# Hybrid diffusion backbone on one core: conditioning dots moved from the attention to the merge, and norms in two VectorE operations per block

## Chip, cores, metric

The kernel runs on one core of one Trainium2 chip. The metric is the device time of one execution in microseconds (us); three runs of the kernel before gave a median of 2265.24 us (2264.16 to 2270.03).

## What is computed

Two layers of a token mixer and an MLP on 512 latent tokens of width 1024, with 256 context tokens as a prefix that goes through the same weights. All is fp32. Cut to what matters here:

```python
for l in range(2):
    mod = silu(c) @ w_ada[l] + b_ada[l]          # 6 x 1024 columns; the same with c_ctx for the context
    sh1, sc1, g1, sh2, sc2, g2 = split(mod, 6)
    h = rms_norm(x, norm1[l]) * (1 + sc1) + sh1
    u, q, k, v, ..., gates = project(h @ w_in[l])
    y_pool, y_swa, y_diff = pool_mixer(u), windowed_gqa(...), diff_attention(...)
    merged = sum(sigmoid(gate_b) * (y_b @ w_b) for b in (pool, swa, diff))
    x = x + g1 * (merged @ w_out[l])
    h2 = rms_norm(x, norm2[l]) * (1 + sc2) + sh2
    x = x + g2 * (relu(h2 @ w_ff1[l])**2 @ w_ff2[l])
    # the context does the same in layer 0
```

The 6144 values of `mod` are 48 columns of 128: 0 to 7 are sh1, 8 to 15 sc1, 16 to 23 g1, 24 to 31 sh2, 32 to 39 sc2, 40 to 47 g2.

## The kernel before

**Layout and precision.** Activations lie transposed: eight blocks of 128 rows of the width, with 768 token columns (512 latent, 256 context). A matmul keeps fp32 precision by three passes: every operand is a pair of tiles, the value rounded to the matmul's format (the high half, written by ScalarE) and the remainder (the low half, a subtraction). The products high x high, low x high and high x low go into one PSUM tile (lines 231 to 233, 1014 to 1016, 396). Weights stream through SyncE's queue as tiles of 768 columns (`raw`, 384 KB, line 190) and are split into `W` on the way: high half on ScalarE (line 172), low half (line 173) on VectorE, or on GpSimd where the caller passes an engine. Three raw and six split tiles are in flight. A tile holds six weight blocks of 128 x 128.

**Order of the work.** Per layer: first norm, attention (projections, windowed and differential attention, with gate units as filler), pooling branch, merge, output projection with the second norm, MLP. The order in the program is written out by hand (`ORDER`, `unit_plan`, `merge_plan`, `mlp_plan`); the order on each engine is planned from it at build time, with priorities (`PRI`, `HIGH`). Every engine and SyncE's queue then work in their order.

**Conditioning dots.** A column of `mod` is the dot of 128 rows of `w_ada` (a load of 512 KB, tile `wada`) with the activated conditioning vector, one for the latents and, in layer 0, one for the context: `tensor_tensor_reduce` over 1024 columns on VectorE. Columns 0 to 15 of layer 0 are made with matmuls in the prologue. Columns 16 to 39 of layer 0 run beside the attention of layer 0: `ada_attn` (lines 250 to 266, dot at line 264, load at line 262), a generator that `pump()` advances by one column, 24 columns over the first 30 of the attention's steps (line 910). The rest, columns 40 to 47 of layer 0 and all 48 of layer 1, runs in the MLP of layer 0: `ada` (lines 283 to 288, dot at line 279, load at line 270 and kept in program order), pumped by the feed-forward units (lines 1387 and 1395). `ada` first loads both conditioning vectors (`cvec`, line 244) and activates them (lines 238 and 239). Its weights have two buffers, those of `ada_attn` one.

**Merge** (lines 1279 to 1332). Five gate units (eight blocks each, 768 token columns in two groups, 48 matmuls by three passes) and 24 branch units (four blocks, 24 matmuls); each of them already calls `pump()`, which finds nothing to do there today. A branch unit's result is multiplied by its gate and added up on VectorE (lines 1317, 1321, 1324).

**Norms.** `norm_stats` gives the reciprocal root mean square, broadcast over the partitions in a PSUM tile `bc`: squares on ScalarE (line 310), their sum on VectorE (line 311), a sum over partitions by matmul (line 315), the power on GpSimd (line 180), a broadcast by transposes (line 321). `norm` (second norm, to tile `xn`) and `norm_apply` (first norm of layer 1, in place) multiply the eight blocks by `bc` (lines 354, 348). `modulate` then writes the high half of `h` on ScalarE with scale and bias (line 339), applies scale and shift on VectorE (line 340) and makes the low half (line 341) on VectorE for even blocks and on GpSimd for odd ones (`MODP`). The second norm runs in two halves, each behind its half of the output projection, whose results are added to x at line 1354. In layer 1's first norm the latents are normed while the context's last feed-forward units run in layer 0 (`next(mods)`, line 1403); the context's follow behind those. Of these last feed-forward units the weights' low halves, from line 1392, are made on GpSimd (`FE`).

Of the kernel before, what the change touches and what calls it, by code (L numbers as in the profile page):

```python
# [7 lines left out]
F32 = mybir.dt.float32  # L8
F32R = mybir.dt.float32r
BF16 = mybir.dt.bfloat16  # L10
AF = mybir.ActivationFunctionType
ALU = mybir.AluOpType
# [40 lines left out]
def merge_plan(l):  # L53

    g = (START[l] + sum(GATES_AT[l]))
    first = min(24, max(g, 16) + AHEAD)
    seq = [("gate", i) for i in range(g, first)]
    for i in range(24):
        if i >= 16 and first < 24:
            seq.append(("gate", first))  # L60
            first += 1
        seq.append(("br", i))
    return seq
# [45 lines left out]
HIGH = 100  # L109
OUTA = 1  # L110
OUTE = (None, None)
MODP = 2
PRE = ((0, 0), (0, 4))
YP = ()
MGP = ()
WG = (None, None)
WB = ((None, None), (None, None))
ATT = {"Q": 5, "E": 4, "PT": 3, "y": 2, "ph": 2, "zs": 3, "st": 6, "wada": 1}
ADA_ATTN = range(16, 40)
ADA_STEPS = 30  # L120
KVB = 6
MT = 4
ZC = True
FE = "pool"
LAG = 1
PW = "pool"
RAW = 3
# [8 lines left out]
class Kern:  # L136
# [196 lines left out]
            gs[:, k:k + 2], self.mod[l][:, v, j0 + k:j0 + k + 2], 1.0, self.col(l, norm0 + k, 2),  # L333
            ALU.add, ALU.mult)

    def modulate(self, t, h, k, a, b, gs, sh):

        nc = self.nc
        nc.scalar.activation(h[k][:, 0, a:b], t, AF.Identity, bias=sh[:, k:k + 1], scale=gs[:, k:k + 1])
        nc.vector.tensor_scalar(t, t, gs[:, k:k + 1], sh[:, k:k + 1], ALU.mult, ALU.add)  # L340
        (nc.gpsimd if k % MODP == 1 else nc.vector).tensor_tensor(
            h[k][:, 1, a:b], t, h[k][:, 0, a:b].bitcast(F32), op=ALU.subtract)

    def norm_apply(self, x, a, b):

        bc = self.norm_stats(x, a, b)
        for k in range(8):
            self.nc.vector.tensor_tensor(x[k][:, a:b], x[k][:, a:b], bc[:, 0:b - a], op=ALU.mult)

    def norm(self, x, h, a, b, gs, sh):  # L350
        bc = self.norm_stats(x, a, b)
        for k in range(8):
            t = self.T("xn")[:, 0:b - a]
            self.nc.vector.tensor_tensor(t, x[k][:, a:b], bc[:, 0:b - a], op=ALU.mult)
            self.modulate(t, h, k, a, b, gs, sh)

    def new_h(self, name, pool=None):
        return [(pool or self.hp).tile([128, 2, NT], F32R, tag="h", name=f"{name}{k}") for k in range(8)]
# [472 lines left out]
    def attention(self, l, h, tail):  # L831
# [53 lines left out]

        self.side = self.ada_attn(ADA_ATTN) if l == 0 else None
        for ti in range(6):
# [4 lines left out]
        for gi, (kind, i) in enumerate(items):  # L892
# [13 lines left out]
            for j, (a, subs) in enumerate(us):  # L906
                step(b, a, dd, subs, total * (j + 1) // len(us) - total * j // len(us))
                dd, b = b, a
                done += 1
                self.pump(done * len(ADA_ATTN) // ADA_STEPS - (done - 1) * len(ADA_ATTN) // ADA_STEPS)  # L910
            if gi == len(items) - 2:
# [287 lines left out]
    def run(self):  # L1199
        nc, tc, a, ctx = self.nc, self.tc, self.a, self.ctx  # L1200
        pool = lambda name, bufs=1, **kw: ctx.enter_context(tc.tile_pool(name=name, bufs=bufs, **kw))
# [31 lines left out]
        with tc.manual_schedule():  # L1233
            h = self.prologue(p0.__enter__())
        self.side = None
        prev_pool = p0
        x = None

        def first_norm(l, x, h, v):
            ga, gb = (lat, cx)[v]  # L1240
            gs = self.gains(l, v, 8, 0)
            self.norm_apply(x, ga, gb)
            yield
            for k in range(8):
                self.modulate(x[k][:, ga:gb], h, k, ga, gb, gs, self.mod[l][:, v, 0:8])
                yield

        for l in range(DEPTH):
# [3 lines left out]
            if l > 0:  # L1252
                d = self.first = self.group_w(l, "swa", 0, None)
                if PRE:
                    with tc.issue_after(self.last_mm.ins):
                        for t, k in PRE:
                            self.proj_mm(l, h, d, t, k, k + 4)
                for _ in first_norm(l, x, h, 1):
                    pass
# [21 lines left out]
            B = _Tagged(raw, {"tg": 8, "mg": 8})  # L1281
            self.tp = _Tagged(raw, {"T": 2})
            mg = [None] * 8
            mh = None
            tg = {}

            def gate(i):
                ps = self.s("gate")
                self.unit(ps, self.blocks(l, "gate", i, eng=WG[l]), h, groups)
                t = tg[i] = B.tile([128, NT], F32, tag="tg", name="tg")  # L1290
                nc.scalar.activation(t[:, 0:n], ps[:, 0:n], AF.Tanh, scale=0.5)
                self.pump()

            def tg_load(i):
                t = tg[i] = B.tile([128, NT], F32, tag="tg", name="tgl")
                nc.sync.dma_start(t[:, 0:n], self.tgd[i][:, 0:n])

            for name, i in merge_plan(l):
                if name == "gate":
                    gate(i)  # L1300
                    continue
                b, m = divmod(i, 8)
                if m == 0:
                    y = self.load_y((0, 2, 1)[b], n)
                    if b == 2:
                        mh = self.new_h("mh")
                if i < (START[l] + sum(GATES_AT[l])):
                    tg_load(i)
                if True:
                    ps = self.s("br")  # L1310
                    self.unit(ps, self.blocks(l, "br", i, eng=WB[l][i % 2]), y, groups)
                    t = tg.pop(i)
                    hi = tc.high_priority(offset=HIGH)
                    hi.__enter__()
                    if b == 0:
                        mg[m] = B.tile([128, NT], F32, tag="mg", name="mg")
                        nc.vector.scalar_tensor_tensor(mg[m][:, 0:n], t[:, 0:n], 1.0, ps[:, 0:n],
                                                       ALU.add, ALU.mult)
                        hi.__exit__(None, None, None)
                    else:  # L1320
                        nc.vector.scalar_tensor_tensor(t[:, 0:n], t[:, 0:n], 1.0, ps[:, 0:n],
                                                       ALU.add, ALU.mult)
                        hi.__exit__(None, None, None)
                        (nc.gpsimd if b in MGP else nc.vector).tensor_tensor(mg[m][:, 0:n], mg[m][:, 0:n], t[:, 0:n],
                                                                             op=ALU.add)
                    self.pump()
                    if b == 2:
                        nc.scalar.activation(mh[m][:, 0, 0:n], mg[m][:, 0:n], AF.Copy, scale=0.5)
                        nc.vector.scalar_tensor_tensor(mh[m][:, 1, 0:n], mg[m][:, 0:n], 0.5,
                                                       mh[m][:, 0, 0:n].bitcast(F32), ALU.mult, ALU.subtract)  # L1330
            pb.__exit__(None, None, None)
            pk.__exit__(None, None, None)

# [5 lines left out]
            x = []  # L1339
            for k in range(8):  # L1340
                t = M.tile([128, NT], F32, tag="x", name="x")
# [6 lines left out]
            for turn, (ga, gb) in enumerate(halves):  # L1348
                v = turn if l == 0 else 0
# [7 lines left out]
                if l == 0 or turn == 0:  # L1357
                    gs = self.gains(l, v, 32, 8)
                self.norm(x, h2, ga, gb, gs, self.mod[l][:, v, 24:32])
            if l == 0:  # L1360
                pc_ = tc.tile_pool(name=f"pd{l}", bufs=1, reuse_waits="tile")
# [13 lines left out]
            f = {}  # L1375
# [13 lines left out]
            def ff2(i, e, turn, gr):  # L1389
                m = i % 8  # L1390
                ps = self.s("ff2")
                self.unit(ps, self.blocks(l, "ff2", i, eng=FE if turn else None, turn=turn),
                          [f[e, turn, k] for k in range(4)], gr, NL if turn else 0)
# [17 lines left out]
            for name, i, e, turn in plan[4:]:  # L1411
                gr = groups if l > 0 or e < 7 else [cx] if turn else [lat]
                if name == "ff1":
                    if turn and i == 28:
                        self.pump(48)
                        pc_.__exit__(None, None, None)
                        pc_ = tc.tile_pool(name="pf", bufs=1, reuse_waits="tile")
                        fc = _Tagged(pc_.__enter__(), {"f": 4})
                    ff1(i, e, turn, None, gr)
                    continue  # L1420
                ff2(i, e, turn, gr)
                if l == 0 and e == 7 and turn == 0 and i % 8 == 7:
                    for k in range(8):
                        nc.sync.dma_start(xd[k], x[k][:, 0:NL])
                    h = self.new_h("h")
                    mods = first_norm(1, x, h, 0)
                    next(mods)
# [126 lines left out]
```

## Time and profile before

| | |
|---|---|
| median of three runs | 2265.24 us |
| profiled execution | 2268.85 us |
| span of its instructions | 2267.1 us |
| granted TensorE clock, mean | 0.991 |
| busy: TensorE / weight loads / VectorE / ScalarE / GpSimd | 97 / 86 / 67 / 42 / 12 % |

Busy times are unions of instruction spans. The stretches named below are us from the start of the span: layer 0's attention goes to some 575, its merge to some 715, its second norm lies around 765 to 815, its MLP to 1343, layer 1's first norm from 1320 to 1364; layer 1's attention goes to some 1740 and its second norm lies around 1878 to 1918.

### The profile page before, as it was taken

Reading aid. Unit: us, or ns where it says so; the run is one execution under the profiler, and the core shown is the slowest. Engines: PE = TensorE matmul, PEld = TensorE weight load, DVE = VectorE, ACT = ScalarE, POOL = GpSimd, SP = SyncE. Lnnn points to the kernel's source line nnn. Section 1 sums busy time; section 2 is a strip of 40 time slices with the busy share of each in tenths; the row PEclk is TensorE's granted clock in tenths of the full one; section 3 lists DMA queues with packets and bytes.
Section 4 is the critical chain, followed back from the end, with each engine's and each line's share of the span. In section 5 each row is a group of like instructions: output and inputs, shape, how many; then the busy total and the mean of one; then the engine's idle time right before and its main releaser. Section 6 shows DMA issues by size and latency. Waiting matters only on the chain.

```text
span 2267.1 us, 34112 instructions
## 1 busy us (share of the span) xinstructions
PE 2198.7 (97%) x12924; PEld 1960.8 (86%) x12924; DVE 1508.1 (67%) x2899; ACT 963.2 (42%) x1979; POOL 268.2 (12%) x383
## 2 busy tenths in 40 slices
PE   8999999999999999999999989999999999999999
PEld 3988999988888888888888879999998889888887
DVE  5899976687356788655554487766778677454453
ACT  4455655565322442222222254756556435322331
POOL 3212112231000100000000032122221001000000
PEclk9999999999999999999999999999999999999999
DMA  6434322111554344333333242212222654333332
GB/s 253 144 116 135 117 83 69 44 60 60 188 160 147 118 162 151 128 128 128 119 128 106 87 139 71 80 55 84 75 75 83 225 187 125 112 93 96 98 94 74
DMA packets 108810, 260.53 MB, mean 115 GB/s; under 512 B 13027, under 2 KB 33635, under 8 KB 107494
## 3 DMA queue, kind: packets, MB, share of 16 engines
q1 hardware_dynamic: 108646, 258.35, 35.0%
q8 instruction: 102, 1.67, 0.3%
q14 instruction: 62, 0.51, 0.1%
HBM read 233.00 MB, written 25.30 MB: 114 GB/s over the span
## 4 chain that ended last, share of the span: by engine, by line
PE 42%; issue 24%; DVE 9%; ACT 2%; DMA 2%; POOL 1%; SPq 0%; ACTq 0%; POOLq 0%; DVEq 0%
PE ff L233 5%; PE ff L232 5%; PE ff L231 5%; PE z L396 4%; PE br L232 2%; PE br L233 2%; PE br L231 2%; PE gate L1014 2%; PE gate L1015 2%; PE gate L1016 2%; DVE W L173 1%; DMA raw<-in_w_dram 1%; PE out L233 1%; PE out L232 1%; PE out L231 1%
## 5 line engine op out<-in xcount | busy, mean ns | idle before, releaser
L172 ACT ACTIVATE W<-raw 128x768 fp32r<-128x768 f32 (+1 forms) x383 | 320.6, 839 | 599.6 <-PE ff L233 427.6
L173 DVE TENSOR_TENSOR W<-raw,W 128x768 fp32r<-128x768 f32 (+1 forms) x373 | 357.8, 961 | 250.9 <-ACT W L172 246.4
L396 PE MATMUL z<-W,h 128*128 128x384 f32 (+2 forms) x1728 | 312.4, 331 | 8.8 <-ACT h L1098 2.9
L396 PEld LDWEIGHTS z<-W,h 128*128 128x128 f32 x1728 | 286.1, 191 | 12.9 <-ACT h L1098 3.2
L232 PE MATMUL ff<-h,W 128*128 128x512 f32 (+1 forms) x800 | 281.3, 352 | 0.0
L231 PE MATMUL ff<-h,W 128*128 128x512 f32 (+1 forms) x800 | 280.9, 351 | 0.0
L233 PE MATMUL ff<-h,W 128*128 128x512 f32 (+1 forms) x800 | 280.8, 351 | 0.0
L232 PE MATMUL ff<-f,W 128*128 128x512 f32 x736 | 264.2, 359 | 0.1
L231 PE MATMUL ff<-f,W 128*128 128x512 f32 x736 | 263.2, 358 | 0.0
L233 PE MATMUL ff<-f,W 128*128 128x512 f32 x736 | 262.4, 357 | 0.0
L180 POOL TENSOR_TENSOR rs<-ms,mhalf 128x4 f32<-128x4 f32 (+4 forms) x79 | 84.6, 1071 | 1261.4 <-DVE ms L179 1174.1
L1014 PE MATMUL gate<-h,W 128*128 128x256 f32 (+1 forms) x656 | 213.9, 326 | 3.8 <-DVE ob L574 3.8
L1015 PE MATMUL gate<-h,W 128*128 128x256 f32 (+1 forms) x656 | 213.3, 325 | 0.0
L1016 PE MATMUL gate<-h,W 128*128 128x256 f32 (+1 forms) x656 | 210.5, 321 | 0.0
L1399 DVE SCALAR_TENSOR_TENSOR x<-ff,mod,x 128x512 f32<-128x512 f32 (+1 forms) x192 | 121.6, 658 | 108.7 <-PE ff L233 108.6
L231 PEld LDWEIGHTS ff<-h,W 128*128 128x128 f32 x800 | 151.9, 190 | 21.5
L233 PEld LDWEIGHTS ff<-h,W 128*128 128x128 f32 x800 | 151.6, 189 | 21.5
L232 PEld LDWEIGHTS ff<-h,W 128*128 128x128 f32 x800 | 151.6, 190 | 21.4
L231 PEld LDWEIGHTS ff<-f,W 128*128 128x128 f32 x736 | 138.8, 189 | 21.7
L233 PEld LDWEIGHTS ff<-f,W 128*128 128x128 f32 x736 | 138.3, 188 | 21.3
L232 PEld LDWEIGHTS ff<-f,W 128*128 128x128 f32 x736 | 138.6, 188 | 20.8 <-DVE f L1373 0.5
L1014 PEld LDWEIGHTS gate<-h,W 128*128 128x128 f32 x656 | 125.4, 191 | 5.5 <-DVE ob L574 4.8
(266 smaller groups left out, 4527.2 us busy)
## 6 DMA issues: line engine op xcount, KB each, us to landing
raw<-in_w_dram SPq DMA_DIRECT2D x375, 384.0 KB, 3.1
wada<-in_wada_dram SPq DMA_DIRECT2D x80, 512.0 KB, 3.9
wa<-in_wada_dram SPq DMA_DIRECT2D x8, 1024.0 KB, 7.8
tgd<-tgs SPq DMA_DIRECT2D x38, 192.0 KB, 2.1
tgl<-tgd SPq DMA_DIRECT2D x19, 384.0 KB, 3.9
tgd<-tgs SPq DMA_DIRECT2D x44, 128.0 KB, 2.3
tgl<-tgd SPq DMA_DIRECT2D x22, 256.0 KB, 3.9
yl<-yd SPq DMA_DIRECT2D x12, 384.0 KB, 3.8
```

What stands on the lines that cost most here:

```text
L172: nc.scalar.activation(H, src, AF.Copy)
L173: (eng or nc.vector).tensor_tensor(L, src, H.bitcast(F32), op=ALU.subtract)
L180: nc.gpsimd.tensor_tensor(out, t, self.mhalf[:, 0:n], op=ALU.pow)
L231: mm(ps[:, a:b], wh, x[0][:, r], start=k == 0, stop=False)
L232: mm(ps[:, a:b], wh, x[1][:, r], start=False, stop=False)
L233: self.last_mm = mm(ps[:, a:b], wl, x[0][:, r], start=False, stop=k == nk - 1)
L396: self.nc.tensor.matmul(z[:, c0:384], h[k][:, hpart, ts], d["W"][k // 2][:, wpart, (k % 2) * 384 + c0:(k % 2 + 1) * 384], start=(k == 0 an ...
L1014: mm(ps, wh, x[:, 0, a:b], start=k == 0, stop=False)
L1015: mm(ps, wh, x[:, 1, a:b], start=False, stop=False)
L1016: return mm(ps, wl, x[:, 0, a:b], start=False, stop=k == len(acts) - 1)
L1399: nc.vector.scalar_tensor_tensor(x[m][:, ga:gb], ps[:, ga:gb], self.mod[l][:, v, 40 + m:41 + m], x[m][:, ga:gb], ALU.mult, ALU.add)
```

## The change

Columns 24 to 39 of layer 0 leave `ada_attn` and go through `ada` in the merge, in a pool of their own; what the merge's pumps don't reach is pumped at its end. The attention keeps columns 16 to 23, still spread over 30 steps. The norms multiply by the gain and the broadcast factor in one operation (`scaled`); ScalarE adds the shift for the high half, and VectorE adds the shift and subtracts the high half in one operation. All low halves of the norms, and of the weights of the context's last feed-forward, are made on VectorE.

```diff
-MODP = 2
-ADA_ATTN = range(16, 40)
+ADA_ATTN = range(16, 24)
-FE = "pool"
+FE = None
-    def modulate(self, t, h, k, a, b, gs, sh):
+    def modulate(self, t, h, k, a, b, sh):
         nc = self.nc
-        nc.scalar.activation(h[k][:, 0, a:b], t, AF.Identity, bias=sh[:, k:k + 1], scale=gs[:, k:k + 1])
-        nc.vector.tensor_scalar(t, t, gs[:, k:k + 1], sh[:, k:k + 1], ALU.mult, ALU.add)
-        (nc.gpsimd if k % MODP == 1 else nc.vector).tensor_tensor(
-            h[k][:, 1, a:b], t, h[k][:, 0, a:b].bitcast(F32), op=ALU.subtract)
-
-    def norm_apply(self, x, a, b):
+        nc.scalar.activation(h[k][:, 0, a:b], t, AF.Identity, bias=sh[:, k:k + 1])
+        nc.vector.scalar_tensor_tensor(h[k][:, 1, a:b], t, sh[:, k:k + 1], h[k][:, 0, a:b].bitcast(F32),
+                                       ALU.add, ALU.subtract)
+
+    def scaled(self, t, x, k, gs, bc):
+        self.nc.vector.scalar_tensor_tensor(t, x, gs[:, k:k + 1], bc, ALU.mult, ALU.mult)
+
+    def norm_apply(self, x, a, b, gs):
         bc = self.norm_stats(x, a, b)
         for k in range(8):
-            self.nc.vector.tensor_tensor(x[k][:, a:b], x[k][:, a:b], bc[:, 0:b - a], op=ALU.mult)
+            self.scaled(x[k][:, a:b], x[k][:, a:b], k, gs, bc[:, 0:b - a])
     def norm(self, x, h, a, b, gs, sh):
...
-            self.nc.vector.tensor_tensor(t, x[k][:, a:b], bc[:, 0:b - a], op=ALU.mult)
-            self.modulate(t, h, k, a, b, gs, sh)
+            self.scaled(t, x[k][:, a:b], k, gs, bc[:, 0:b - a])
+            self.modulate(t, h, k, a, b, sh)
...
             mg = [None] * 8
+            if l == 0:
+                pc_ = tc.tile_pool(name=f"pc{l}", bufs=1, reuse_waits="tile")
+                self.side = self.ada(pc_.__enter__(), [(0, j) for j in range(24, 40)])
...
+            self.pump(48)
+            if l == 0:
+                pc_.__exit__(None, None, None)
             pb.__exit__(None, None, None)
```

## Rows read from the trace of the kernel before

**Rows 1.** The page, busy time, share and instructions of each engine.
```profile
PE 2198.7 (97%) x12924; PEld 1960.8 (86%) x12924; DVE 1508.1 (67%) x2899; ACT 963.2 (42%) x1979; POOL 268.2 (12%) x383
```
**Rows 2.** Windows: stretch, length, busy by engine (instructions), granted clock, DMA share, GB/s.
```profile
90.00:290.00 200.00, 187.14 (x1196) 179.27 (x1195) 182.27 (x432) 115.45 (x286) 38.51 (x47) 1.00 0.39 123
290.00:390.00 100.00, 99.47 (x641) 97.35 (x640) 69.87 (x169) 57.86 (x150) 24.97 (x40) 1.00 0.25 78
1400.00:1500.00 100.00, 98.79 (x763) 97.92 (x762) 72.23 (x194) 64.61 (x161) 21.76 (x34) 1.00 0.23 69
840.00:880.00 40.00, 40.00 (x230) 35.00 (x229) 38.09 (x61) 7.36 (x9) 0.00 (x0) 1.00 0.59 196
```
**Rows 3.** TensorE's longest waits from 90 to 290 us: total, times, longest.
```profile
PE ptr L735 <- DVE E L722: 3.1, 3, 1.8
PE tr L493 <- DVE rot L482: 2.6, 2, 1.5
```
**Rows 4.** Line 264, the attention's dots: duration ns min/median/max, first and last start.
```profile
L264 DVE CUSTOM_DVE_ANT_0 cvec<-wada,cvec,cols x48: 1244/1280/1729, 78.5 to 280.7; 128x1024 bf16<-128x1024 f32 x48
L264 DVE DVE_READ_ACCUMULATOR2_ANT mod<- x48: 72/83/87, 79.7 to 281.9; 128x1 f32 x48
```
**Rows 5.** The MLP's dots (line 279) in one window; line 270, their loads.
```profile
840.00:860.00 20.00, 12.36 (x19) 1.00 0.60 202
...
L270 SPq DMA_DIRECT2D wada<-in_wada_dram x56: 327/424/1724, 745.6 to 1215.9; - x56
```
**Rows 6.** Windows: the merge of layer 0, columns as in rows 2.
```profile
570.00:670.00 100.00, 99.57 (x567) 87.61 (x567) 44.74 (x51) 27.81 (x36) 0.00 (x0) 1.00 0.59 188
```
**Rows 7.** Groups by form, VectorE, 770 to 790 us: busy, mean ns, idle before.
```profile
L340 DVE TENSOR_SCALAR xn<-xn,gs,mod 128x512 f32<-128x512 f32 x8 | 5.4, 696 | 0.2 <-ACT h L339 0.2
L354 DVE TENSOR_TENSOR xn<-x,bc 128x512 f32<-128x512 f32 x8 | 5.2, 677 | 1.6 <-PE bc L321 1.6
...
L341 DVE TENSOR_TENSOR h<-xn,h 128x512 fp32r<-128x512 f32 x4 | 3.2, 804 | 0.0
```
**Rows 8.** Timeline: start, us; line 340 alone and beside a GpSimd split.
```profile
778.95 0.54 DVE L340 TENSOR_SCALAR xn<-xn,gs,mod 128x512 f32<-128x512 f32 x1
...
1334.31 4.08 POOL L173 TENSOR_TENSOR W<-raw,W 128x768 fp32r<-128x768 f32 x2
...
1336.62 2.06 DVE L340 TENSOR_SCALAR x<-x,gs,mod 128x512 f32<-128x512 f32 x1
```
**Rows 9.** TensorE's waits from 783 to 790 us.
```profile
PE out L231 <- DVE x L1354: 2.2, 2, 1.4
PE out L233 <- DVE W L173: 1.3, 1, 1.3
```
**Rows 10.** Windows beside layer 0's second norm, columns as in rows 2.
```profile
775.00:780.00 5.00, 5.00 (x44) 5.00 (x43) 5.00 (x9) 3.56 (x5) 1.98 (x2) 1.00 0.01 2
790.00:795.00 5.00, 5.00 (x26) 5.00 (x26) 3.13 (x7) 2.19 (x4) 0.00 (x0) 0.53 0.64 221
```
**Rows 11.** Groups by form, VectorE, 1320 to 1365 us.
```profile
L340 DVE TENSOR_SCALAR x<-x,gs,mod 128x512 f32<-128x512 f32 x8 | 6.5, 826 | 0.0
L341 DVE TENSOR_TENSOR h<-x,h 128x512 fp32r<-128x512 f32 x4 | 5.3, 1324 | 0.0
L348 DVE TENSOR_TENSOR x<-x,bc 128x512 f32<-128x512 f32 x8 | 5.2, 678 | 1.8 <-PE bc L321 1.8
```
**Rows 12.** TensorE's longest wait from 1320 to 1370 us.
```profile
PE ssq L315 <- DVE acc L311: 3.9, 1, 3.9
```
**Rows 13.** Groups by form, VectorE, 570 us to the end: nearest prices.
```profile
L173 DVE TENSOR_TENSOR W<-raw,W 128x768 fp32r<-128x768 f32 x313 | 301.1, 963 | 237.3 <-ACT W L172 233.2 <-DMA tgl<-tgd 0.2
...
L1399 DVE SCALAR_TENSOR_TENSOR x<-ff,mod,x 128x512 f32<-128x512 f32 x128 | 95.9, 749 | 108.7 <-PE ff L233 108.6
...
L1354 DVE SCALAR_TENSOR_TENSOR x<-out,mod,x 128x256 f32<-128x256 f32 x24 | 11.4, 479 | 6.5 <-PE out L233 6.4
...
L1329 DVE SCALAR_TENSOR_TENSOR mh<-mg,mh 128x512 fp32r<-128x512 f32 x8 | 5.5, 686 | 0.7 <-ACT mh L1328 0.7
```

More of the change, by code (lines that the diff above doesn't have):

```diff
@@ L1241, in first_norm @@
             gs = self.gains(l, v, 8, 0)
-            self.norm_apply(x, ga, gb)
+            self.norm_apply(x, ga, gb, gs)
             yield
             for k in range(8):
-                self.modulate(x[k][:, ga:gb], h, k, ga, gb, gs, self.mod[l][:, v, 0:8])
+                self.modulate(x[k][:, ga:gb], h, k, ga, gb, self.mod[l][:, v, 0:8])
                 yield
```

## Prediction

> **What bounds the kernel now.** I read the busy line of the page first. TensorE is busy 97% of the span, VectorE 67% [rows 1]: the end is set by TensorE's work, and a change that touches none of it can only give back what TensorE idles. So the question is where TensorE idles, and whether the change reaches those places. The windows say where. In layer 0's attention, from 90 to 290 us, TensorE has 187.14 us busy of 200 while VectorE has 182.27 (91%). From 290 to 390, still attention but after the last dot, TensorE has 99.47 of 100 with VectorE at 70%. The sliding-window part of layer 1, which has no dots, has 98.79 of 100 with VectorE at 72%. In the feed-forward stretch 840 to 880 VectorE is busier still (95%), yet TensorE has 40.00 of 40: there long matmul chains wait for no short VectorE step [rows 2]. So a full VectorE costs time only in the attention and around the norms. The list of TensorE's waits says the same for 90 to 290: the longest are on short steps of VectorE, such as the scaled exponentials and the rope sum [rows 3].
>
> I sum against the profiled execution: 2268.85 us, span 2267.1, so 1.75 us lie outside. It is 3.6 us above the median of 2265.24. What a measurement can tell from no change is about 0.3%, 6.8 us.
>
> **Columns 24 to 39 leave the attention.** Today 48 dots run there, the first at 78.5 us, the last at 280.7, each 1.28 us plus 0.083 us for its accumulator, 1.363 together [rows 4]. Sixteen columns for two vectors are 32 dots: 43.6 us of VectorE leave. Sixteen loads of 512 KB leave SyncE's queue there too; the load and activation of the conditioning vectors stay. VectorE then has 182.3 - 43.6 = 138.7 us to do in that stretch, 74% of some 187 us, close to the 70 and 72% of the two comparison stretches [rows 2]. At their TensorE share (0.991 between them) the same matmuls take 187.14 / 0.991 = 188.8 us: 11.2 us less. Matmul spans overlap and hide short stops; weight-load time is a sharper measure: 179.27 us, against shares of 0.974 and 0.979 in the comparison stretches, gives 179.27 / 0.976 = 183.7 us: 16.3 us less. The low bound is 0, if the waits come from the length of the chains and not from the queue on VectorE. I take 12, near the first value, because 16 dots remain. The trace shows no attention unit of layer 0 with exactly this load.
>
> The Trainium skill, Perfetto Trace Analysis, section Identifying the Most-Contended Engine, says that TensorE's matmul occupancy is a bad measure and that weight-load occupancy should be taken. By that rule the term is 16.3 instead of 12; the two stretches of rows 2 do show weight loads falling by 8 points where matmul occupancy falls by 5.
>
> **They arrive in the merge.** There are 29 pumps (5 gate units, 24 branch units) and 16 columns, so the dots are issued with the first 16 units: 4 gates of 48 matmuls and 12 branches of 24, at 567 matmuls in 100 us [rows 6] some 85 us. Added to VectorE: 43.6 us, and about 2.6 us for doubling the two conditioning vectors, at the price of a dot, which has the same 1024 columns. ScalarE gets two tanh, taken as costing no more than that, where it has 27.81 us busy of 100. VectorE has 44.74 of 100 there [rows 6], 38 in those 85 us; with 46 more it is full, and some dots slip into the units behind. The precedent is 840 to 860: 12.36 us of dots in 20 us [rows 5], VectorE 95% full over the 40 us [rows 2], TensorE without a gap; the merge would get 46 in 85, or 10.9 in 20, no denser. So I cost it at nothing; the cover is the weight tiles split ahead and the long units. On SyncE's queue 16 loads of 512 KB and one of 1 MB join the weight, gate and branch-output loads: 9.4 MB, about 110 GB/s beside 188. The same loads stand between weight loads in the feed-forward, 56 of them [rows 5]. The load of the conditioning vectors may wait for memory of the attention's last tiles; behind it stand weight loads, again with tiles split ahead. Bounds 0 and +5 us within the forecast; the cover gone, more, as rival (c).
>
> **The norms.** Per block of 128 rows before: multiply by the broadcast factor (L354, L348), scale and shift (L340), and on every second block the low half (L341) on VectorE, the others on GpSimd. After: two operations with a scalar and two tensors per block, all on VectorE. The first reads PSUM as L1399 does, 0.749 us for 512 columns; the second reads SBUF as L1329 does, 0.686 [rows 13]. For the 512 columns of a latent norm: 8 x (0.749 + 0.686) = 11.5 us.
>
> Layer 0's second norm today: 8 x 0.696 + 8 x 0.677 + 4 x 0.804 = 14.2 us [rows 7]. The saving is 2.7 us. The scale-and-shift is slow beside GpSimd: alone 0.54 us, beside a GpSimd split 2.06 [rows 8]. Here it counts, because output-projection results and weight splits queue behind the norm on VectorE: TensorE waits 2.2 + 1.3 = 3.5 us for them [rows 9] and then runs at the lower of its two levels (granted 0.53, near 1.2 GHz): 26 matmuls in 5 us instead of 44 [rows 10], 5 x 18/44 = 2.0 us lost. I take 2.7 of the wait and half of the clock: 3.7 us. Ends 0 and 5.5.
>
> The Trainium skill, VectorE: DVE Perf Modes, section The perf-mode tier table, speaks against this edit: an fp32 operation with one tensor in SBUF can run at twice the rate of one with two tensors, so the removed scale-and-shift is the cheap kind and the new operations are not. With the uncontended 0.54 of rows 8 the saving would be 1.5 us instead of 2.7; the trace's mean of 0.696 decides.
>
> Layer 1's first norm, latent half, runs beside the context's last feed-forward: 8 x 0.826 + 8 x 0.678 + 4 x 1.324 = 17.3 us today [rows 11], 11.5 after, 5.8 less. But the splits of those 32 weight blocks come back from GpSimd: 32/6 = 5.3 tiles x 0.963 [rows 13] = 5.1 us on VectorE. Net 0.7 less. The context's half has 256 columns, so about half of layer 0's saving, 1.4 us. These lie on the path: TensorE has nothing left and waits 3.9 us for the sum of squares behind VectorE's queue [rows 12]. Other VectorE instructions stretched by GpSimd there shorten too, so I take 2.5. Ends: 5 less (nothing stretched any more), 3 more (splits late for the context's matmuls).
>
> Layer 1's second norm: two halves of 256 columns, at 0.479 us per PSUM operation [rows 13]; the first is covered by output-projection matmuls, and after the second TensorE has feed-forward units of the first half. Nothing; 1 us either way. GpSimd loses its low halves and nobody waits for what it keeps.
>
> Sum: -12 + 0 - 3.7 - 2.5 = -18.2 us: 2250.6 for an execution like the profiled one, and from the median 2265.24 - 18.2 = **2247 us**.
>
> **Rivals.** (a) Attention waits on chains, not on VectorE: the steps of a unit follow one another through four engines, so a shorter queue buys nothing. For it: VectorE is not full, and the two comparison stretches do other work. Against: the jump from 94 to 99% where the dots end [rows 2]. Then only the norms gain: 2265.24 - 6.2 = 2259, or 2262 with part of their lower ends. (b) All terms at their good end: -16.3 - 5.5 - 5 = -26.8: 2238. (c) Slower: a branch unit of the merge is 24 matmuls, 4.2 us [rows 6]; its two dots are 2.7 us beside 1.9 of VectorE's own (44.74 of 100), 4.6 together. If the dots stand ahead of the weight splits in VectorE's order, each of 12 branch units overruns, by 0.4 us on average and 1 us at worst; TensorE stops, drops to the lower level as in rows 10 and loses about 1.7 us more (4.2 x 18/44): 12 x 2.7 = 32 us, 2247 + 32 = 2279. It turns slower than before from seven such units (18.2 / 2.7). Against it: 840 to 860 does the same without a gap. (d) The dots slip: the order of each engine is planned from priorities, and the loads' buffers (two) can hold columns back until the second norm needs 24 to 39. They have 100 us of slack; if it fails, the norm waits some 10 us for the last columns (7 dots), and the gain falls to 8: 2257, at the border.
>
> **Chances.** Forecast 0.60, (a) 0.14, (b) 0.14, (c) 0.08, (d) 0.04. Faster by over 0.3% means under 2258.4: the forecast, (b) and some of (d): 0.76. Within 0.3%: (a) and the rest of (d): 0.16. Slower: 0.08. The range takes in (b) with 3 us for the spread of runs and (a): 2235 to 2262.
>
> **What would show it.** Right: TensorE busy share 90 to 290 near 0.99 and weight loads near 0.97; the merge without a TensorE gap at VectorE 90 to 100%; no GpSimd subtraction in the norms and no L340-like outlier of 2 us; a latent norm near 11.5 us of VectorE; granted clock 1.00 around 790. Wrong: attention still at 94%, TensorE waiting for weight splits in the merge, or for the factors of the second norm.

## The result, and the profile after

The changed kernel takes 2243.43 us (median of four runs, 2240.71 to 2244.8) against 2267.64 us for the kernel before beside it (four runs): ratio 0.9894, 95% interval 0.9878 to 0.991, or 24.2 us less. The prediction was 2247.0 us in a range of 2235 to 2262. The profiled execution took 2242.5 us (span 2240.4), 26.4 less than the one of before.

The page's busy line after the change, to be read against [rows 1]:

```profile
PE 2188.2 (98%) x12924; PEld 1952.9 (87%) x12924; DVE 1501.9 (67%) x2883; ACT 961.6 (43%) x1981; POOL 232.2 (10%) x353
```

TensorE does the same 12924 matmuls; VectorE's total hardly moved. Windows of the kernel after, columns as in [rows 2], and under them the first 50 us of that stretch in the kernel before:

```profile
90.00:140.00 50.00, 45.01 (x279) 42.67 (x278) 46.13 (x112) 28.25 (x75) 10.43 (x9) 1.00 0.44 130
140.00:190.00 50.00, 50.00 (x337) 49.24 (x337) 37.80 (x93) 32.36 (x74) 9.73 (x13) 1.00 0.22 66
...
90.00:290.00 200.00, 194.90 (x1269) 189.56 (x1268) 154.54 (x380) 122.85 (x304) 38.89 (x50) 1.00 0.28 84
290.00:390.00 100.00, 100.00 (x637) 98.10 (x637) 70.64 (x171) 57.64 (x156) 26.02 (x41) 1.00 0.26 79
570.00:670.00 100.00, 97.75 (x557) 85.18 (x557) 87.20 (x125) 27.13 (x33) 0.00 (x0) 1.00 0.78 258
...
90.00:140.00 50.00, 44.15 (x275) 42.30 (x274) 45.27 (x104) 27.38 (x75) 10.16 (x9) 1.00 0.40 130
```

From 90 to 290 us TensorE has 73 matmuls more than in [rows 2], and what it still lacks lies nearly all in the first 50 us, where VectorE is as full as before (46.13 us busy against 45.27, the last line). The attention's 16 dots are not spread over its steps; they run first (line 263):

```profile
L263 DVE CUSTOM_DVE_ANT_0 cvec<-wada,cvec,cols x16: 1256/1278/1627, 78.4 to 147.2; 128x1024 bf16<-128x1024 f32 x16
```

The merge has 557 matmuls in 100 us where [rows 6] has 567. TensorE's only wait there, and its waits around layer 0's second norm (740 to 800 us):

```profile
PE br L231 <- DVE y L172: 2.2, 1, 2.2
...
PE bc L320 <- POOL rs L179: 1.8, 2, 1.2
PE out L230 <- ACT sq L309: 0.4, 1, 0.4
PE out L232 <- DVE W L172: 0.3, 1, 0.3
```

Of the 2.2 + 1.3 us of [rows 9] 0.3 is left, and the clock no longer falls behind the norm, as the windows of its latent half and of the time after it show (before: [rows 10]; the last window has fewer matmuls because the feed-forward's, with 512 columns each, have begun):

```profile
763.00:768.00 5.00, 5.00 (x44) 5.00 (x43) 4.80 (x8) 3.10 (x5) 0.00 (x0) 1.00 0.01 3
768.00:773.00 5.00, 4.32 (x34) 3.94 (x33) 5.00 (x9) 2.52 (x5) 0.00 (x0) 1.00 0.02 2
773.00:778.00 5.00, 5.00 (x44) 5.00 (x43) 4.17 (x9) 2.59 (x5) 0.00 (x0) 1.00 0.72 238
778.00:783.00 5.00, 4.73 (x26) 3.76 (x26) 4.04 (x7) 2.78 (x5) 0.00 (x0) 1.00 0.81 227
```

The norm's operations by form, VectorE, 750 to 776 us (layer 0's second norm; before: [rows 7]), then 1300 to 1346 us (layer 1's first; before: [rows 11]):

```profile
L339 DVE SCALAR_TENSOR_TENSOR h<-xn,mod,h 128x512 fp32r<-128x512 f32 x8 | 5.5, 745 | 0.0
L344 DVE SCALAR_TENSOR_TENSOR xn<-x,gs,bc 128x512 f32<-128x512 f32 x8 | 5.5, 742 | 1.6 <-PE bc L320 1.6
...
L339 DVE SCALAR_TENSOR_TENSOR h<-x,mod,h 128x512 fp32r<-128x512 f32 x8 | 5.9, 746 | 0.0
L344 DVE SCALAR_TENSOR_TENSOR x<-x,gs,bc 128x512 f32<-128x512 f32 x8 | 5.6, 742 | 0.8 <-PE bc L320 0.8
```

Where the time came from, by the first TensorE matmul of each stage in the two profiled executions (us):

| stretch | before | after | difference |
|---|---|---|---|
| to the merge's first gate unit | 577.9 | 562.0 | -15.9 |
| merge to output projection, layer 0 | 143.4 | 145.8 | +2.4 |
| output projection and second norm, layer 0 | 76.5 | 70.8 | -5.7 |
| MLP, layer 0 | 545.0 | 544.1 | -0.9 |
| first norm, layer 1 (to the first transpose) | 25.7 | 23.8 | -2.0 |
| rest of layer 1 (to the last matmul) | 894.5 | 889.9 | -4.6 |

The last row gathers small differences of stages in which little was changed. In the kernels below that have the changed kernel's code for these stages this row goes from 887.3 to 896.8 us, so its -4.6 cannot be put down to the change; where those differences come from was not settled.

### The profile page after: what moved, and what is told of

Read it like the earlier page. It is cut to its first block, busy times and chain, and to the rows that moved or that the text cites. A ratio compares the mean times of both kernels' runs of the same rounds, so it can differ in the third digit from the quotient of the medians.

```text
span 2240.4 us, 34089 instructions
## 1 busy us (share of the span) xinstructions
PE 2188.2 (98%) x12924; PEld 1952.9 (87%) x12924; DVE 1501.9 (67%) x2883; ACT 961.6 (43%) x1981; POOL 232.2 (10%) x353
## 4 chain that ended last, share of the span: by engine, by line
PE 65%; DVE 7%; DMA 3%; ACT 2%; issue 2%; POOL 1%; SPq 0%; POOLq 0%; ACTq 0%; DVEq 0%
PE ff L231 13%; PE ff L230 13%; PE ff L232 13%; PE z L398 4%; PE br L231 2%; PE br L232 2%; PE br L230 2%; DMA raw<-in_w_dram 2%; PE gate L1016 2%; PE gate L1018 2%; PE gate L1017 2%; DVE W L172 1%; PE out L232 1%; PE out L231 1%; PE out L230 1%
## 5 line engine op out<-in xcount | busy, mean ns | idle before, releaser
L172 DVE TENSOR_TENSOR W<-raw,W 128x768 fp32r<-128x768 f32 (+2 forms) x379 | 360.8, 954 | 231.4 <-ACT W L171 226.6
L278 DVE CUSTOM_DVE_ANT_0 junk<-wada,cbc,cols 128x1024 bf16<-128x1024 f32 x112 | 143.4, 1280 | 47.8 <-DMA wada<-in_wada_dram 47.4
L232 PEld LDWEIGHTS ff<-f,W 128*128 128x128 f32 x736 | 138.4, 188 | 21.3
```

Source lines behind the costliest of these rows:

```text
L172: (eng or nc.vector).tensor_tensor(L, src, H.bitcast(F32), op=ALU.subtract)
L232: self.last_mm = mm(ps[:, a:b], wl, x[0][:, r], start=False, stop=k == nk - 1)
L278: self.nc.vector.tensor_tensor_reduce(junk, w, c[:, v, :], 0.5, self.col(l, 21 + j), ALU.mult, ALU.add, self.mod[l][:, v, j:j + 1])
```

## Experiments

In these, "start of the merge" is the first gate matmul, read as for the table above.

**The two halves alone.** Into the kernel before, first only the move of the dots (the diff's lines for `ADA_ATTN` and the merge's pool and pump), then only the norms (`scaled`, `modulate`), with the last feed-forward's splits still on GpSimd.

> Only the dots move; norms and weight splits stay as before. Theory (the gain of the attention comes from VectorE's queue and is separate from the norms): the merge starts some 16 us earlier than before (562 instead of 578 us), its branch units take 2.5 us more for one late split, and nothing changes behind: 13 us less than before in all, ratio 0.994. Rival (the attention gains because the whole order was planned anew, or only together with the norms): the merge starts less than 8 us earlier.

> Only the norms change; the dots stay in the attention and the low halves of the context's last feed-forward weights stay on GpSimd. Theory: the stretch from the output projection's start to the feed-forward of layer 0 loses 5.7 us as in the changed kernel, with TensorE at full clock around its second norm; the second norm of layer 1 gives 1 to 3 us, its first norm 2 to 4: 8 to 12 us less than before, ratio 0.996. Rival (the stretch gained because the dots before it were gone or moved): 4 us or less.

Dots alone: 2251.7 us, ratio 0.9941 (0.992 to 0.9962), merge at 561.6. The gain is the expected one, with one miss: no wait in the merge, which lasts as long as before, although it holds the same dots as in the changed kernel. Norms alone: 2253.35 us, 0.995 (0.9934 to 0.9965); output projection and second norm of layer 0 take 70.8 us as in the changed kernel, so that gain does not hang on the dots. The two gains, 13.5 and 11.9 us below the 2265.21 of before, add up to 25.4; both together gave 24.2.

**GpSimd's part.** Into the kernel before, only the splits of the last feed-forward units on VectorE:

```diff
-FE = "pool"
+FE = None
```

> Only the splits of the context's last feed-forward weights move from GpSimd to VectorE. Theory (GpSimd's work stretches VectorE's two-tensor operations by about as much as the splits cost VectorE): within 2 us of before, and the norm's scale-and-shift there falls from a mean of 826 ns to near 700. Rival (VectorE's extra 5 us lie on the path): 3 to 6 us more than before.

Measured 2266.2 us, ratio 1.0008 (0.9996 to 1.0021). Its operations by form in layer 1's first norm (1320 to 1366 us):

```profile
L348 DVE TENSOR_TENSOR x<-x,bc 128x512 f32<-128x512 f32 x8 | 5.1, 681 | 0.8 <-PE bc L321 0.8
L341 DVE TENSOR_TENSOR h<-x,h 128x512 fp32r<-128x512 f32 x4 | 4.2, 1056 | 0.0
...
L340 DVE TENSOR_SCALAR x<-x,gs,mod 128x512 f32<-128x512 f32 x8 | 4.1, 535 | 0.0
```

With no GpSimd split beside it line 340 falls from the 826 ns of [rows 11] to 535, yet the stage takes 28.9 us in place of 25.7: in it the splits that came back cost more than the stretching they had caused. The total is within 2 us of before, as the theory had it, because other stages came out shorter; the stage's 3.2 us are the rival's. In the norms-only kernel, with the splits on GpSimd, the stage takes 21.3 us, although its low halves are stretched (1320 to 1366 us):

```profile
L339 DVE SCALAR_TENSOR_TENSOR h<-x,mod,h 128x512 fp32r<-128x512 f32 x8 | 8.6, 1088 | 0.0
```

So of the changed kernel's -2.0 us in this stage, -4.4 is the norm and +2.5 the splits.

**Fewer operations, or GpSimd out of the way?** The kernel before with its three operations a block, all low halves on VectorE:

```diff
-        (nc.gpsimd if k % MODP == 1 else nc.vector).tensor_tensor(
+        nc.vector.tensor_tensor(
```

> The kernel before with its three operations per block in the norms, but all low halves of the norms on VectorE. Theory (the norms gain by the number of VectorE operations): VectorE's work in a latent norm is 8 x 0.54 + 8 x 0.68 + 8 x 0.69 = 15.3 us against 14.2 before, so the stretch from output projection to feed-forward of layer 0 is not shorter than 75 us (before 76.5, changed 70.8), total within 3 us of before. Rival (they gain because GpSimd no longer stretches VectorE): 73 us or less there, total 4 to 8 us less than before.

Measured 2265.9 us, 0.9996 (0.9986 to 1.0007). By form, 770 to 790 us:

```profile
L341 DVE TENSOR_TENSOR h<-xn,h 128x512 fp32r<-128x512 f32 x8 | 5.2, 683 | 0.0
L354 DVE TENSOR_TENSOR xn<-x,bc 128x512 f32<-128x512 f32 x8 | 5.2, 679 | 2.1 <-PE bc L321 2.1
L340 DVE TENSOR_SCALAR xn<-xn,gs,mod 128x512 f32<-128x512 f32 x8 | 4.1, 540 | 0.0
```

TensorE's waits from 783 to 792 us:

```profile
PE out L233 <- DVE W L173: 2.4, 1, 2.4
PE out L231 <- DVE x L1354: 0.5, 1, 0.5
```

Uncontended but 15.2 us long (8 x (683 + 679 + 540) ns), the norm makes TensorE wait as before, and output projection and norm take 77.3 us. Layer 0's gain comes from two operations in place of three, 11.9 us.

**How many dots in the attention?** The changed kernel with 16 columns left in the attention (the diff below; the merge then gets 32 to 39), and with none, `range(16, 16)` (the merge gets all 24).

```diff
-ADA_ATTN = range(16, 24)
+ADA_ATTN = range(16, 32)
```

> The changed kernel with 16 columns in the attention and 8 in the merge (changed: 8 and 16; before: 24 and 0). Theory (each dot taken out of VectorE's full queue shortens the attention): the merge starts between the two others, at 567 to 573 us. Rival (chance of the planned order): it starts near 562 or near 578, or beyond.

> The changed kernel with no dots in the attention and 24 columns in the merge. Theory: once VectorE has air the rest gives less, so the merge starts 1 to 6 us before the changed kernel's 562; the merge, with 24 columns in 29 units, loses 4 us or more to late low halves. Rival for the attention (every dot costs its own length): 22 us of dots gone, start near 540 to 550. Rival for the merge (density does not matter): a loss of 2.5 us or less.

Single runs of 2259.01 and 2246.22 us. With 16 columns the merge starts at 575.9, near the 577.9 of before: a miss, and what its rival said. With none it starts at 555.8. The window of the kernel without any dot there:

```profile
90.00:290.00 200.00, 199.14 (x1304) 194.68 (x1303) 143.00 (x358) 125.84 (x311) 37.29 (x52) 1.00 0.25 73
```

All the loss of [rows 2] in the attention's first half is then gone, 108 matmuls more than before in the same 200 us. The merge takes 3.6 us more than before's 143.4, but only 1.2 more than the changed kernel's. That the kernel as a whole gains nothing on the changed one comes from further behind: the rest of layer 1, whose code is the same in both, takes 896.8 us against 889.9. Why is not shown.

**Full VectorE, or the dots' place in its order?** So far the dots always ran as early as they could. Now their loads stay in program order, which spreads them: in the kernel before (24 columns), and in the changed one (8).

```diff
-            nc.sync.dma_start(w, self.a["wada"][j - 16])
+            dma = nc.sync.dma_start(w, self.a["wada"][j - 16])
+            self.tc.keep_in_program_order(dma)
```

> The kernel before, all 24 columns still in the attention, with one edit: the load of each column stays in program order, so that the dots are spread over the attention's steps in place of running as early as they can (in the kernels so far they run at 13 to 17 us of dots in each 50 us until they are used up, at 147, 220 or 281 us for 8, 16 or 24 columns). Theory: attention loses time where the dots fill VectorE, in so many us of full VectorE, not by the number of dots. Then no stretch of 50 us has over 11 us of dots, VectorE stays under 88% from 140 to 390 us, weight loads there rise by some 3%, and the merge's first gate unit starts at 564 to 573 us in place of 578. Rival: the number of dots costs, wherever in the attention they stand: the merge starts at 576 to 579 as before, and the end stays within 3 us of before.

> The changed kernel with the same edit, for the 8 columns that it leaves in the attention: their loads stay in program order. Theory (full VectorE costs, not the number): the loss of some 5 us from 90 to 140 us goes, TensorE is busy 49 of 50 us there, the merge starts at 556 to 560 us in place of 562, and the end comes 2 to 6 us earlier than in the changed kernel. Rival (number of dots): the merge starts at 561 to 563 and the end stays where it was.

With 24 columns: 2274.8 us, ratio 1.003 (1.0018 to 1.0043), merge at 583.8. The dots did spread, to at most 10.2 us in 50, and VectorE was never over 85% busy from 140 to 390 us. The theory fell, beyond its rival: TensorE lost more than before. Windows of this kernel, columns as in [rows 2]:

```profile
90.00:390.00 300.00, 282.81 (x1786) 274.07 (x1784) 237.93 (x564) 170.41 (x429) 61.19 (x83) 0.98 0.32 97
...
320.00:325.00 5.00, 0.67 (x4) 0.38 (x3) 5.00 (x13) 1.49 (x4) 0.00 (x0) 0.83 0.49 160
325.00:330.00 5.00, 5.00 (x18) 5.00 (x18) 1.60 (x6) 0.93 (x3) 1.76 (x3) 0.50 0.08 16
```

TensorE's longest group of waits from 90 to 575 us, VectorE's from 80 to 450, and the same wait of VectorE in the kernel before:

```profile
PE tr L494 <- DVE rot L483: 9.5, 4, 4.3
...
DVE cvec L265 <- DMA wada<-in_wada_dram: 12.1, 14, 1.7
...
DVE cvec L264 <- DMA wada<-in_wada_dram: 8.6, 10, 1.7
```

A dot that waits for its load holds all of VectorE's queue, 12.1 us in 14 cases; that time is not in VectorE's busy share. It was 8.6 us before, so it is a small part of the difference. TensorE's longest wait, 4.3 us up to 324.8, on VectorE's timeline (start, duration):

```profile
320.85 0.87 DVE L625 SCALAR_TENSOR_TENSOR E<-E,c 128x256 f32<-128x256 f32 x2
321.64 1.27 DVE L265 CUSTOM_DVE_ANT_0 cvec<-wada,cvec,cols 128x1024 bf16<-128x1024 f32 x1
322.84 0.08 DVE L265 DVE_READ_ACCUMULATOR2_ANT mod<- 128x1 f32 x1
322.84 1.27 DVE L265 CUSTOM_DVE_ANT_0 cvec<-wada,cvec,cols 128x1024 bf16<-128x1024 f32 x1
324.05 0.08 DVE L265 DVE_READ_ACCUMULATOR2_ANT mod<- 128x1 f32 x1
324.05 0.28 DVE L482 TENSOR_TENSOR rot<-rg,t 128x128 f32<-128x128 f32 x1
324.25 0.41 DVE L483 TENSOR_TENSOR rot<-rg,t 128x256 f32<-128x256 f32 x1
```

A pair of dots, 2.4 us of the 4.3, stands ahead of two short rope sums of 0.3 and 0.4 us for which TensorE is waiting; TensorE then runs 5 us at a granted 0.50, its lower level (1.2 GHz). With 8 columns spread: 2245.07 us, 0.99 (0.9885 to 0.9915), merge at 561.6. The loss of the first 50 us is gone, as the theory wanted, but smaller ones have come in the later stretches, and the sum is the rival's:

```profile
90.00:140.00 50.00, 48.97 (x312) 47.77 (x311) 36.62 (x91) 30.93 (x82) 10.29 (x12) 1.00 0.30 88
140.00:190.00 50.00, 49.21 (x330) 48.09 (x329) 35.23 (x88) 30.82 (x71) 9.88 (x12) 1.00 0.21 66
190.00:240.00 50.00, 49.53 (x317) 48.12 (x316) 39.53 (x99) 32.11 (x87) 12.17 (x17) 1.00 0.29 87
```

All starts of the merge against the 555.8 without dots (555.6 and 556.2 in the two last kernels below, which have none there either): 16 dots cost 6.2 us early and 5.8 spread, 32 cost 20.0, 48 cost 22.1 early and 27.9 spread. That is 0.36 to 0.63 us of TensorE's time for a dot of 1.36 us, wherever in the attention it stands. The edit also changes the planned order of other instructions, so the single values carry that too; why 32 cost nearly as much as 48 stays open.

**The merge's dots.** The changed kernel with a column for every second branch unit only, then the same with the splits of the last feed-forward back on GpSimd (`FE = "pool"`):

```diff
-                    self.pump()
+                    if i % 2 == 0:
+                        self.pump()
```

> The changed kernel with a pump on every second branch unit of the merge, so that its dots come half as densely there. Theory (the changed kernel's merge loses 2.5 us because VectorE, full with dots, makes the low half of a branch input late): TensorE has no gap in the merge and the kernel takes 2 to 3 us less than the changed one, about 2241. Rival (that stop comes from the loads or is there at any density): the same 2243.

> The changed kernel with a pump on every second branch unit and the last context weight splits on GpSimd again. Theory (moving those splits to VectorE costs its stretch 2.5 us, and the dense dots one stop of 2.4): 3 to 5 us less than the changed kernel timed beside it, and the stretch from layer 1's first projection to its first transposes near 21.3 us (changed 23.8). Rival (both are noise of one profile): the same as the changed kernel within 2 us.

The first: 2244.28 us, 0.9908 (0.9883 to 0.9933); the second: 2243.25 us, 0.9888 (0.9872 to 0.9905). The merge's stop goes in both and layer 1's stage falls to 21.3 us in the second, as the theory had it, but neither median is clearly below the changed kernel's. Output projection and second norm take 71.8 and 72.4 us, 1.0 and 1.6 more, which gives back a part; the profiled executions are 2 us shorter, and differences of that size are within the spread of the runs (2240.03 to 2249.02 us in the first).

Last, no column in the attention, two with each gate unit, one with every second branch unit and with the last four; then with `FE = "pool"`:

```diff
-                self.pump()
+                self.pump(2)
...
-                    self.pump()
+                    if i % 2 == 0 or i >= 20:
+                        self.pump()
```

> The changed kernel with no column left in the attention: all 24 go to the merge, two columns with each of the five gate units, one with every second branch unit and the rest at its end. Theory (a pair of dots in VectorE's queue costs TensorE time wherever it stands ahead of a short step of the attention's chains, and nothing between the long units of the merge): the merge starts at 555 to 557 us in place of 562, takes 109.7 to 111 us, and the median falls 4 to 8 us below the changed kernel's, to a ratio of 0.986 to 0.988 to before. Rival (VectorE's work comes back wherever it is put): the merge or the output projection behind it takes 4 us or more longer, and the ratio stays at 0.989 to 0.991.

> The kernel of the run before, and the weights' low halves of the context's last feed-forward units back on GpSimd. Theory (these splits cost layer 1's first norm 2.5 us on VectorE): that stage takes 21 to 22 us in place of 24, and the ratio is 0.985 to 0.987. Rival (what a stage gains the next ones give back, as with the merge's columns spread): within 1.5 us of the run before.

The first: 2248.04 us, 0.9917 (0.9903 to 0.993), 4.6 us above the changed kernel, though the intervals of the two ratios touch. The attention gives its 6 us (merge at 556.2) and the merge takes 0.9 us more than before's 143.4, but the dots at its end now delay the merged rows: output projection and norm take 76.2 us, 5.4 more than in the changed kernel. TensorE's wait:

```profile
PE out L231 <- DVE mh L1335: 3.3, 1, 3.3
```

VectorE's timeline around it (start, duration), with a dot ahead of and one behind the last merged rows `mh` (more dots and merged rows stand in what is left out):

```profile
695.02 1.28 DVE L278 CUSTOM_DVE_ANT_0 junk<-wada,cbc,cols 128x1024 bf16<-128x1024 f32 x1
...
701.43 0.95 DVE L1335 SCALAR_TENSOR_TENSOR mh<-mg,mh 128x768 fp32r<-128x768 f32 x1
702.30 0.95 DVE L1329 TENSOR_TENSOR mg<-mg,tg 128x768 f32<-128x768 f32 x1
703.17 0.95 DVE L172 TENSOR_TENSOR W<-raw,W 128x768 fp32r<-128x768 f32 x1
704.05 1.29 DVE L278 CUSTOM_DVE_ANT_0 junk<-wada,cbc,cols 128x1024 bf16<-128x1024 f32 x1
```

In this stage it is as the rival had it. The ratio lies a little above the rival's range, and not through the dots' new place alone: merge, output projection and norm give back 3.9 of the attention's 5.8 us, while the MLP takes 2.5 us more and the rest of layer 1, whose code is the changed kernel's, 896.8 us against 889.9. The second: 2242.86 us, 0.9897 (0.9884 to 0.9911), layer 1's stage 21.7 us against 23.8 in the first; the stage is as the theory had it. The total is 5.2 us below the run before, which is more than the stage's 2.1, because the rest of layer 1 takes 891.1 us this time; neither the theory's ratio nor the rival's 1.5 us came out. None of these kernels is measurably faster than the changed one.

## Why the prediction was right, and where not

**Attention, -12 with ends 0 and -16.3: measured -15.9.** The term was mis-sized by choosing a value near the matmul share over the weight-load share of [rows 2], "because 16 dots remain". The Trainium skill, Perfetto Trace Analysis, section Identifying the Most-Contended Engine, prefers weight-load occupancy; this case's trace agrees in so far as that measure's 16.3 is nearer than 11.2. That it almost meets 15.9 is luck: both shares price the loss from all 48 dots, of which 16 stayed. These cost 6.2 us, so the full loss was 22.1, more than either share gave. The signs named for a right prediction were met in part: the clock behind the norm is 1.00, but from 90 to 290 us TensorE's share is 0.97 and that of weight loads 0.95, where 0.99 and 0.97 were named, and the merge has one gap.

The mechanism behind the number was only half right. The step "a full VectorE costs time only in the attention" read [rows 2] as a matter of VectorE's share. From 90 to 390 us VectorE was busy 237.93 us with the dots spread and 252.14 in the kernel before, yet TensorE's busy time was 282.81 against 286.61 (the sums of [rows 2] for before). VectorE's waits for the dots' loads in that window, 9.4 and 7.1 us, do not turn this round. What the runs show in its place is the queue: a dot of 1.3 us, or a pair, ahead of a short step for which TensorE waits. This is seen in single waits such as the one above; that all of the loss arises so is inferred from the cost per dot, which is of one size early and spread. Rival (a) had the place of the waits right, the chains, and its conclusion wrong: without dots the same chains leave TensorE 199.14 of 200 us busy. The assumption of an even 74% from 90 to 290 us fell too: the dots run first, in a stretch that stays 92% full (46.13 of 50).

**Merge, 0 with ends 0 and +5: +2.4 in the profile.** Inside the bounds. The precedent of [rows 5] did not carry: the merge has an operand that the feed-forward units looked at there don't have, the second branch's output `y`, which must be split before its first unit. From 621.5 to 633.1 us six dots stand between VectorE's other work, and `y`'s low halves come behind them (VectorE's timeline):

```profile
631.03 0.95 DVE L1322 SCALAR_TENSOR_TENSOR mg<-tgl,br 128x768 f32<-128x768 f32 x1
631.89 1.28 DVE L278 CUSTOM_DVE_ANT_0 junk<-wada,cbc,cols 128x1024 bf16<-128x1024 f32 x1
633.10 0.08 DVE L278 DVE_READ_ACCUMULATOR2_ANT mod<- 128x1 f32 x1
633.10 1.82 DVE L172 TENSOR_TENSOR y<-yl,y 128x768 fp32r<-128x768 f32 x2
```

Rival (c) named this mechanism but had it in each of 12 units; it came once. The same dots with the old norms and splits (the dots-only kernel) show no such wait, so it hangs on the planned order; what tips that was not settled. Rival (d) fell: the last dot of the merge starts at 650.3 us, 100 us ahead of the norm.

**Layer 0's second norm, -3.7 with end -5.5: measured -5.7.** The norm took 11.9 us of VectorE for 11.5 predicted: the operation with both tensors in SBUF costs 745 ns, not the 686 of [rows 13]. Even so 3.2 us of the 3.5 of wait went, and with it the whole fall of the clock; half of the 2.0 was counted. The Trainium skill, VectorE: DVE Perf Modes, section The perf-mode tier table, spoke against the edit: for 2048 columns it lists the kind of operation that was removed at twice the rate of one with two tensors. Its direction holds here at 512 columns: uncontended, the scale-and-shift took 540 ns against 679 and 683 for operations with two tensors, a ratio of 0.8 and not a half. With all three operations uncontended (15.2 us) nothing was gained, so what decides here is that one operation a block is gone.

**Layer 1's first norm, -2.5: measured -2.0.** Made of -4.4 and +2.5 where the prediction had -5.8 - 1.4 and +5.1: both were sized too large, the splits twofold; what hides the rest of them was not tried. **Layer 1's second norm**, 0 ± 1: the stage fell from 50.2 to 49.0 us, but it is 48.2 to 49.1 in the dots-only, splits-only and spread-24 kernels, which leave it as it was, so nothing is shown of it.

**The sum** was -18.2, the medians gave -24.2. The attention explains 3.9 of the 6.0 and the norm 2.0, against 2.4 of the merge and 0.5 of layer 1's first norm; what is left, 3.0, lies in small differences that no run here pins to a part, among them the table's last row. That these fell on the good side is luck.

## What to carry to other kernels

Do not price background work on an in-order engine by that engine's busy share: look at what stands right behind each piece in its queue, and whether another engine is waiting for it. Put long pieces where only long units depend on the queue, and keep them clear of the places where an operand is handed over (a new input's split, the last rows of a stage). Where a norm lies on the path, fewer operations per block beat offloading one of three; and an offload to GpSimd is worth keeping only where it takes more off VectorE than it stretches. Before a gain or loss of a few microseconds is put down to an edit, look at how far stages that the edit doesn't touch move between the same kernels.

## What the runs showed of the hardware, unexpected

- GpSimd subtractions beside VectorE stretch VectorE's own operations unevenly: the 512-column scale-and-shift averages 826 ns with them and 535 without; a low half with both tensors in SBUF 1088 against 746; the multiply that reads PSUM stays at 678 to 681.
- The operation with a scalar and two tensors takes the same time with one tensor in PSUM (742 ns) as with both in SBUF (745), and 476 to 480 ns for 256 columns.
- A wait of TensorE of 4.3 us was followed by 5 us at the lower clock level, at half the full clock: up to 2.5 us of work lost on top of the wait. In [rows 9] and [rows 10] it is much the same behind three shorter ones, 3.5 us together: a granted 0.53 for 5 us.
